# Attention in a two-layer backbone: p times v for four heads in one product, split into high and low parts

## The chip, the cores and the metric

The kernel runs on one core of a Trainium2 chip. The time is that of one execution on the device, in microseconds, as the median of several runs. The engines are named as the profile names them: PE is TensorE (matrix products and transposes into PSUM), PEld its loading of weights, DVE is VectorE, ACT is ScalarE, POOL is GpSimd, and SP issues most of the transfers. Each engine works through its own list of instructions in order and waits on semaphores of the others.

## The reference, cut to what matters

The program is one step of a backbone with two layers, for 128 context tokens and 256 latent tokens. Layer 0 is a gated MLP beside a state-space scan; layer 1, which the change touches, is grouped-query attention with 16 query heads, 4 key/value heads and heads of 128:

```python
def one_block(qblk):
    s = jnp.einsum('bqkgd,bskd->bkgqs', qblk, k).astype(jnp.float32) * scale
    p = jax.nn.softmax(s, axis=-1).astype(v.dtype)
    return jnp.einsum('bkgqs,bskd->bqkgd', p, v)
```

Context queries see the 128 context keys. Latent queries see 384 keys: 128 from a cache and 256 latent ones with rotary applied. The attention's output is multiplied by a SiLU gate z and goes through the output projection. Everything is fp32.

## The kernel before

Tokens are held as three tiles of 128 (t = 0 is the context, t = 1 and 2 the latents). The large products are done in fp32r in three parts: each fp32 operand is split into a high part (a copy to fp32r on ACT) and a low part (the difference, on DVE; `split`, line 274), and three products hi x hi, lo x hi, hi x lo are summed. Weights come as units of 128x1024 (`raw`), are split into `wh` and `wl` one or two units ahead of their use (`advance`, line 320), and four such pairs exist.

Layer 1 runs as follows. The keys' and values' projections come first. Then, for each of four groups g (one key/value head, four query heads), `xstat` does q's projection (512 columns per product) and `wstat` the gate z's (four units of 384 columns). The attention of the groups is worked in between: it is written as Python generators, and the planner runs one step of what is ready after every triple of projection products (`tick`, line 210), judged by a rough clock of its own that holds each engine's time; a step is taken 2.3 us of that clock after its inputs are due. The order in which steps are emitted is then kept on every engine.

One head of a (group, tile) pair is `head_gen` (line 1625): the scores on PE (`sm<-kT,qT`), the maximum on DVE (`mx`), the exponential with its sum on ACT (`p`), the reciprocal and the scaling on DVE, transposes of p on PE (`sm<-cm,p`, one per key block, so three for a latent tile and one for the context), a copy of them to SBUF on ACT (`pT`), and one fp32 product per key block on PE (`mm<-pT,vv`) into a quarter of a PSUM bank that the pair's four heads share (`po`). Up to three heads are under way at once (`attn_gen`). After the fourth head the bank is gated (`of<-mm,zs`, DVE) and split for the output projection (`aH` on ACT, `aL` on DVE).

Two places wait for the attention: the output projection may start once groups 0 to 2 are done, and its second block of columns takes its banks once group 3 is done (`until(...)` and `bank()` at the end of `build`). Where the planner must wait there, it goes on emitting steps of the attention with no projection product between them. Banks of PSUM: five for products (`mm`), three for scores and transposes (`sm`).

Of the kernel before, what the change touches and what calls it, by code (L numbers as in the profile page):

```python
# [8 lines left out]
F32 = mybir.dt.float32  # L9
F32R = mybir.dt.float32r  # L10
AF = mybir.ActivationFunctionType
# [5 lines left out]
P = 128  # L17
NT = 3
T = NT * P
# [156 lines left out]
def build(tc, A, O):  # L176
    nc = tc.nc
    clock = Clock()
    V, S, G, PE, SP = (Timed(e, n, clock) for e, n in (
        (nc.vector, "V"), (nc.scalar, "S"), (nc.gpsimd, "G"), (nc.tensor, "PE"), (nc.sync, "SP")))  # L180
    BF16 = mybir.dt.bfloat16
    with ExitStack() as ctx:
        def pool(name, bufs=1, space=None, st=ctx, **kw):
            if space is not None:
                kw["space"] = space
            return Slots(st.enter_context(tc.tile_pool(name=name, bufs=bufs, **kw)), name, bufs, clock)
# [17 lines left out]
        kept_bank = [0]  # L204
# [34 lines left out]
        def bank():  # L239
            until(lambda: live[0] + kept_bank[0] < MM)  # L240
            return any_bank()
# [5 lines left out]
        def free():  # L247
            live[0] -= 1

        def smt():  # L250
            until(lambda: sm_free)
            sm_free.remove(min(sm_free))
            return sm.tile([P, 512], F32, name="sm")

        def take():
            while not sm_free or min(sm_free) > clock.at["PE"] + SLACK:
                yield
            return smt()

        def give(ps):  # L260
            sm_free.append(clock.last(ps))
# [12 lines left out]
        def split(r, h, l):  # L274
            S.activation(h, r, AF.Copy)
            V.tensor_sub(l, r, h.bitcast(F32))
# [209 lines left out]
        def bc(ap, shape):  # L486
            return ap.to_broadcast(shape)
# [273 lines left out]
        while mod_at or w_at or rb or any(queue.values()):  # L761
# [3 lines left out]
            if xts:  # L765
                t, q = xts[0]
# [25 lines left out]
            elif what == "rb":  # L792
                b = min(rb)
# [405 lines left out]
        pss = [bank() for _ in range(NT)]  # L1199
# [3 lines left out]
        for q in range(1, 4):  # L1203
            pss = [bank() for _ in range(NT)]
# [33 lines left out]
        for n in range(4):  # L1238
            pss = [bank() for _ in range(NT)]
# [20 lines left out]
        for n in range(4):  # L1260
            pss = [bank() for _ in range(NT)]
# [55 lines left out]
        pss = [bank() for _ in range(NT)]  # L1317
# [26 lines left out]
        for n in range(1, 3):  # L1344
            pss = [bank() for _ in range(NT)]
# [61 lines left out]
        pss = {t: bank() for t in (0, 1)}  # L1407
# [27 lines left out]
        pss = {t: bank() for t in (0, 1)}  # L1435
# [35 lines left out]
        def k_norm(pl, t, ps):  # L1471
            ss = small.tile([P, 4], F32, name="ss")
            jk = pl.tile([P, P], BF16, name="jk", bufs=2 if pl is pb else 1)
            for h in range(4):
                S.activation(jk, ps[:, h * P:(h + 1) * P], AF.Square, accum_out=ss[:, h:h + 1])
            rk[t] = rstd(ss, P, 4)
# [22 lines left out]
        pk = pool("pk", 1, st=st)  # L1499
        pa = pool("pa", 1, st=st)  # L1500
        kT = pk.tile([P, 4, 4 * P], F32, name="kT")
        vv = pk.tile([P, 4, 512], F32, name="vv")
        SP.dma_start(out=kT[:, :, P:2 * P], in_=A["ckT"])
        SP.dma_start(out=vv[:, 1], in_=A["cv"])
        qkn = pk.tile([P, 2, P], F32, name="qkn")
        SP.dma_start(out=qkn, in_=A["qkn"].partition_broadcast(P))
        kq = pa.tile([P, 4, T], F32, name="zs", bufs=2)
# [1 line left out]
        def k_out(t, ps):  # L1509
            V.tensor_tensor(kq[:, :, t * P:(t + 1) * P], ps.rearrange("p (h c) -> p h c", h=4),  # L1510
                            bc(rk[t].unsqueeze(2), [P, 4, P]), op=ALU.mult)
            free()
# [5 lines left out]
        def make_tab():  # L1518
            rot = pa.tile([P, 2, 2, P], F32, name="of", bufs=1)
            SP.dma_start(out=rot, in_=A["rot"])  # L1520
            for w in (1, 0):
                G.tensor_tensor(tab[:, w, 0], rot[:, 0], bc(qkn[:, w].unsqueeze(1), [P, 2, P]), op=ALU.mult)
                q4 = qkn[:, w].rearrange("p (a b c) -> p a b c", a=2, b=2)
                for b in range(2):
                    G.tensor_tensor(tab[:, w, 1].rearrange("p t (a b c) -> p t a b c", a=2, b=2)[:, :, :, b],
                                    rot[:, 1].rearrange("p t (a b c) -> p t a b c", a=2, b=2)[:, :, :, b],
                                    bc(q4[:, :, 1 - b].unsqueeze(1), [P, 2, 2, 32]), op=ALU.mult)
                yield
# [26 lines left out]
        def k_seq(ps):  # L1555
            yield
            k_norm(pa, 2, ps)
            yield rk[2]
            k_out(2, ps)
            yield from make_tab()  # L1560
            yield tab
            for t in range(NT):
                c = 0 if t == 0 else (t + 1) * P
                yield from rope(kq[:, :, t * P:(t + 1) * P], t, 1, lambda: kT[:, :, c:c + P], ("k", t))
            flags.add("k done")
# [3 lines left out]
        def v1_gen(pss):  # L1569
            yield  # L1570
            for t in range(NT):
                S.activation(vv[:, 0 if t == 0 else t + 1], pss[t], AF.Copy)
                free()
            SP.dma_start(out=O[5], in_=vv[:, 0])
            flags.add("vv")

        pss = [bank() for _ in range(NT)]
# [42 lines left out]
            free()  # L1620
            flags.add(("z", g, h))

        heads, po, done = [0], {}, {}

        def head_gen(g, t, h):
            k0, nk = (0, 1) if t == 0 else (1, 3)
            w = nk * P
            ps = yield from take()
            PE.matmul(ps[:, :w], qT[g, t][:, h], kT[:, g, k0 * P:k0 * P + w], start=True, stop=True)
            if h == 3:  # L1630
                flags.add(("sc", g, t))
            mx = small.tile([P, 4], F32, name="mx", bufs=6)
            V.reduce_max(mx[:, 0:1], ps[:, :w], AX.X)
            V.tensor_scalar_mul(mx[:, 0:1], mx[:, 0:1], -scale)
            p = pa.tile([P, T], F32, name="p", bufs=3)
            S.activation(p[:, :w], ps[:, :w], AF.Exp, scale=scale, bias=mx[:, 0:1], accum_out=mx[:, 1:2])
            give(ps)
            yield p
            V.reciprocal(mx[:, 2:3], mx[:, 1:2])
            V.tensor_scalar_mul(p[:, :w], p[:, :w], mx[:, 2:3])  # L1640
            yield p
            pt = yield from take()
            for i in range(nk):
                PE.transpose(pt[:, i * P:(i + 1) * P], p[:, i * P:(i + 1) * P], ident)
            pT = pa.tile([P, 3, P], F32, name="pT", bufs=3)
            S.activation(pT[:, 0:nk], pt[:, :w].rearrange("p (a b) -> p a b", a=nk), AF.Copy)
            give(pt)
            yield pT
            if (g, t) not in po:
                while live[0] >= MM:  # L1650
                    yield
                po[g, t] = any_bank()
                kept_bank[0] = 0
                done[g, t] = 0
            for i in range(nk):
                PE.matmul(po[g, t][:, h * P:(h + 1) * P], vv[:, k0 + i, g * P:(g + 1) * P], pT[:, i],
                          start=i == 0, stop=i == nk - 1)
            heads[0] -= 1
            done[g, t] += 1
            if done[g, t] == 4:  # L1660
                while not has(*[("z", g, i) for i in range(4)]):
                    yield
                ts = slice(t * P, (t + 1) * P)
                of = pa.tile([P, 4, P], F32, name="of", bufs=1)
                V.scalar_tensor_tensor(of, po[g, t].rearrange("p (h c) -> p h c", h=4), 0.5,
                                       zst[g][:, :, ts], op0=ALU.mult, op1=ALU.mult)
                free()
                kept_bank[0] = int((3, NT - 1) not in po and all(x == 4 for x in done.values()))
                kept_bank[0] = int((3, NT - 1) not in po and len(po) == sum(x == 4 for x in done.values()))
                split(of, oH[:, 4 * g:4 * g + 4, ts], oL[:, 4 * g:4 * g + 4, ts])  # L1670
                flags.add(("attn", g, t))

        def attn_gen():
            while not has("vv", ("k", 0), ("k", 1), ("k", 2)):
                yield
            for g in range(4):
                for t in range(NT):
                    while ("q", g, t) not in flags:
                        yield
                    for h in range(4):  # L1680
                        while heads[0] >= 3:
                            yield
                        heads[0] += 1
                        spawn(head_gen(g, t, h))
                        yield
# [3 lines left out]
        for g in range(4):  # L1689
            pss = [bank() for _ in range(NT)]  # L1690
# [8 lines left out]
        pss = [bank() for _ in range(NT)]  # L1699
# [49 lines left out]
        pss = [bank() for _ in range(NT)]  # L1749
# [3 lines left out]
        pss = [bank() for _ in range(NT)]  # L1753
# [132 lines left out]
```

## Time and profile before

| | us |
|---|---|
| median of 3 runs | 1836.07 |
| lowest and highest run | 1833.1, 1837.0 |
| the profiled execution, its own time | 1834.68 |
| its span, first to last instruction | 1832.9 |
| PE busy in the span | 1776.6 |
| DVE busy | 1264.2 |
| ACT busy | 739.8 |

The mean granted clock of TensorE over the span is 0.991 of full speed. A busy time of PE is a sum of instructions whose ends are modelled, since products are pipelined; how long a product takes in a stream is better read from the distance between the starts of two that follow each other. In the timeline an fp32 product of 128 columns leaves two records.

### The profile page before, as it was taken

What the parts mean: (1) busy time and instruction counts of PE and PEld (TensorE: products, weight loads), DVE (VectorE), ACT (ScalarE), POOL (GpSimd) and SP (SyncE); (2) the same over time, 40 slices, a digit from 0 to 9 for tenths busy, and PEclk for the clock granted to TensorE, in tenths of its full rate; (3) what the DMA queues carried; (4) which work ended last, traced back from release to release, by engine and by line L of the source; (5) the groups of instructions that cost most, each with busy time, mean ns of one, the idle gap of its engine ahead of it and who ended that gap; (6) DMA issues with size and microseconds to landing.
All of it is one profiled execution on the core that took longest, in us unless ns stands there. A gap on an engine that the chain in (4) does not pass through costs nothing.

```text
span 1832.9 us, 24975 instructions
## 1 busy us (share of the span) xinstructions
PE 1776.6 (97%) x9332; PEld 1545.8 (84%) x9332; DVE 1264.2 (69%) x2023; ACT 739.8 (40%) x1380; POOL 203.4 (11%) x247
## 2 busy tenths in 40 slices
PE   6999998899999999999999999998999999999998
PEld 3579888899998888889999999877789898988876
DVE  4325888687768787777788878775566776776454
ACT  3224564566444332233233233244534344444441
POOL 0000134343222000000000000021311010000000
PEclk9999999999999999999999999999999999999999
DMA  9883455455434565776666656675454444434483
GB/s 359 340 309 128 140 171 160 126 146 154 153 127 138 183 205 170 224 213 206 214 204 210 209 188 210 216 243 195 148 190 154 138 150 150 149 127 149 138 286 116
DMA packets 109832, 340.86 MB, mean 186 GB/s; under 512 B 11920, under 2 KB 29840, under 8 KB 108560
## 3 DMA queue, kind: packets, MB, share of 16 engines
q1 hardware_dynamic: 109248, 339.18, 56.5%
q8 instruction: 73, 1.20, 0.3%
q14 instruction: 47, 0.39, 0.1%
q10 hardware_dynamic: 464, 0.10, 0.0%
HBM read 330.19 MB, written 9.04 MB: 185 GB/s over the span
## 4 chain that ended last, share of the span: by engine, by line
PE 83%; DVE 7%; ACT 3%; DMA 3%; issue 2%; POOL 1%; DVEq 0%; POOLq 0%; SPq 0%; ACTq 0%
PE mm L155 72%; PE sm L155 11%; DMA raw<-in_wout_dram 2%; DVE wl L155 2%; ACT wh L155 1%; DVE hb L155 1%; DVE acc L155 1%; DVE v L155 1%; DVE cv L155 1%; DMA raw<-in_mod_dram 0%; ACT hH L155 0%; ACT jk L155 0%; DMA gn<-gate 0%; DMA x<-in_x_dram 0%; DVE EE L155 0%
## 5 line engine op out<-in xcount | busy, mean ns | idle before, releaser
L155 DVE TENSOR_TENSOR wl<-raw,wh 128x1024 fp32r<-128x1024 f32 x358 | 440.7, 1238 | 301.8 <-ACT wh L155 301.2
L155 ACT ACTIVATE wh<-raw 128x1024 fp32r<-128x1024 f32 x358 | 375.7, 1056 | 488.2 <-DMA raw<-in_win_dram 195.0
L155 PE MATMUL mm<-hH,wh 128*128 128x384 f32 x1200 | 423.5, 353 | 3.8 <-DVE xpad L155 3.8
L155 PE MATMUL mm<-hH,wl 128*128 128x384 f32 x1200 | 404.3, 337 | 0.9 <-DVE wl L155 0.9
L155 PE MATMUL mm<-hL,wh 128*128 128x384 f32 x1200 | 403.7, 336 | 0.0
L155 DVE SCALAR_TENSOR_TENSOR acc<-raw,scol,acc 128x512 f32<-128x512 f32 x480 | 335.9, 760 | 15.1 <-DMA raw<-in_mod_dram 14.6
L155 PE MATMUL mm<-wh,hH 128*128 128x512 f32 x636 | 262.3, 412 | 6.1 <-DVE zs L155 4.0
L155 PE MATMUL mm<-wh,hL 128*128 128x512 f32 x636 | 249.7, 393 | 0.6 <-POOL hL L155 0.6
L155 PE MATMUL mm<-wl,hH 128*128 128x512 f32 x636 | 249.0, 392 | 0.0
L155 PEld LDWEIGHTS mm<-hH,wh 128*128 128x128 f32 x1200 | 227.1, 189 | 23.1 <-issue 20.5
L155 PEld LDWEIGHTS mm<-hL,wh 128*128 128x128 f32 x1200 | 227.2, 189 | 1.9
L155 PEld LDWEIGHTS mm<-hH,wl 128*128 128x128 f32 x1200 | 226.6, 189 | 2.1 <-DVE wl L155 2.1
L155 PE MATMUL mm<-wh,aL 128*128 128x512 f32 x504 | 196.6, 390 | 0.0
L155 PEld LDWEIGHTS mm<-wh,hH 128*128 128x128 f32 x636 | 120.3, 189 | 32.1 <-DVE zs L155 4.4
L155 PEld LDWEIGHTS mm<-wh,hL 128*128 128x128 f32 x636 | 119.9, 189 | 27.0 <-POOL hL L155 1.1
L155 PEld LDWEIGHTS mm<-wl,hH 128*128 128x128 f32 x636 | 120.4, 189 | 24.2
L155 PE MATMUL mm<-wl,r 128*128 128x512 f32 x348 | 136.2, 391 | 1.9 <-DVE wl L155 1.9
L155 PE MATMUL mm<-wh,r 128*128 128x512 f32 x348 | 136.8, 393 | 0.8 <-ACT wh L155 0.8
L155 POOL TENSOR_TENSOR rs_r<-rs_t,nhalf 128x1 f32<-128x1 f32 (+1 forms) x54 | 42.7, 791 | 642.1 <-DVE rs_t L155 641.8
L155 PEld LDWEIGHTS mm<-wh,aL 128*128 128x128 f32 x504 | 94.6, 188 | 19.6
L155 DVE SCALAR_TENSOR_TENSOR cv<-xpad,convw,cv 128x386 f32<-128x386 f32 x128 | 82.9, 651 | 2.3
L155 PEld LDWEIGHTS mm<-wl,r 128*128 128x128 f32 x348 | 65.3, 188 | 17.0 <-DVE wl L155 3.9
(257 smaller groups left out, 2084.4 us busy)
## 6 DMA issues: line engine op xcount, KB each, us to landing
raw<-in_win_dram SPq DMA_DIRECT2D x273, 512.0 KB, 4.0
raw<-in_mod_dram SPq DMA_DIRECT2D x128, 512.0 KB, 3.9
raw<-in_wout_dram SPq DMA_DIRECT2D x104, 512.0 KB, 4.3
aL<-in_mod_dram SPq DMA_DIRECT2D x52, 512.0 KB, 8.2
cb<-cumd SPq DMA_DIRECT2D x32, 384.0 KB, 5.5
wide<-in_mod_dram SPq DMA_DIRECT2D x12, 512.0 KB, 9.8
gn<-gate SPq DMA_DIRECT2D x8, 512.0 KB, 6.0
x<-in_x_dram SPq DMA_DIRECT2D x3, 1024.0 KB, 7.3
```

Of the source, the lines that this page charges most:

```text
L155: i = f(*a, **kw)
```

## The change

The probabilities of the four heads of one (group, tile) pair are transposed and split into `pH` and `pL`, which lie in one tile `[P, 2, 3, 4, P]`, heads side by side. Once all four are there, three fp32r products of 512 columns per key block give the whole bank. The values are kept as `vH` and `vL` in place of `vv`; the cached values are loaded into a scratch tile and split, and the context's values are copied once more for the output. There is one such pair of tiles, so the next pair's transposes come after the products of this one; there are two buffers of p in place of three, and two heads are under way at once in place of three. The program's scratch setting (`dynamic_dma_scratch_size`) goes from 4096 to 1024 bytes, which leaves more of SBUF for tiles.

```diff
-        vv = pk.tile([P, 4, 512], F32, name="vv")
+        vH = pk.tile([P, 4, 512], F32R, name="vH")
+        vL = pk.tile([P, 4, 512], F32R, name="vL")
-        SP.dma_start(out=vv[:, 1], in_=A["cv"])
+        cv = pa.tile([P, 512], F32, name="ro", bufs=1)
+        SP.dma_start(out=cv, in_=A["cv"])
...
+            yield cv
+            split(cv, vH[:, 1], vL[:, 1])
...
-                S.activation(vv[:, 0 if t == 0 else t + 1], pss[t], AF.Copy)
+                b = 0 if t == 0 else t + 1
+                split(pss[t], vH[:, b], vL[:, b])
+                if t == 0:
+                    vo = pa.tile([P, 512], F32, name="pT", bufs=1)
+                    S.activation(vo, pss[t], AF.Copy)
+                    SP.dma_start(out=O[5], in_=vo)
                 free()
-            SP.dma_start(out=O[5], in_=vv[:, 0])
...
-            p = pa.tile([P, T], F32, name="p", bufs=3)
+            p = pa.tile([P, T], F32, name="p", bufs=2)
...
+            if (g, t) not in pTs:
+                while pTs:
+                    yield
+                tl = pa.tile([P, 2, 3, 4, P], F32R, name="pT", bufs=1)
+                pTs[g, t] = tl[:, 0], tl[:, 1]
+                done[g, t] = 0
+            pH, pL = pTs[g, t]
             pt = yield from take()
             for i in range(nk):
                 PE.transpose(pt[:, i * P:(i + 1) * P], p[:, i * P:(i + 1) * P], ident)
-            pT = pa.tile([P, 3, P], F32, name="pT", bufs=3)
-            S.activation(pT[:, 0:nk], pt[:, :w].rearrange("p (a b) -> p a b", a=nk), AF.Copy)
+            split(pt[:, :w].rearrange("p (a b) -> p a b", a=nk), pH[:, 0:nk, h], pL[:, 0:nk, h])
             give(pt)
-            yield pT
-            if (g, t) not in po:
+            heads[0] -= 1
+            done[g, t] += 1
+            if done[g, t] == 4:
+                yield (pH[:, 0:nk], pL[:, 0:nk])
                 while live[0] >= MM:
                     yield
                 po[g, t] = any_bank()
                 kept_bank[0] = 0
-                done[g, t] = 0
-            for i in range(nk):
-                PE.matmul(po[g, t][:, h * P:(h + 1) * P], vv[:, k0 + i, g * P:(g + 1) * P], pT[:, i],
-                          start=i == 0, stop=i == nk - 1)
-            heads[0] -= 1
-            done[g, t] += 1
+                for i in range(nk):
+                    mh, ml = (x[:, i].rearrange("p h c -> p (h c)") for x in (pH, pL))
+                    wh, wl = (x[:, k0 + i, g * P:(g + 1) * P] for x in (vH, vL))
+                    PE.matmul(po[g, t], wh, mh, start=i == 0, stop=False)
+                    PE.matmul(po[g, t], wh, ml, start=False, stop=False)
+                    PE.matmul(po[g, t], wl, mh, start=False, stop=i == nk - 1)
+                del pTs[g, t]
...
-                        while heads[0] >= 3:
+                        while heads[0] >= 2:
...
-    nc = _bacc.Bacc("TRN2", target_bir_lowering=False, num_devices=1, dynamic_dma_scratch_size=4096)
+    nc = _bacc.Bacc("TRN2", target_bir_lowering=False, num_devices=1, dynamic_dma_scratch_size=1024)
```

The order of PE's instructions follows. Names: `hH`, `hL`, `aH`, `aL` are activations, `wh`, `wl` weights, `p` the probabilities (transposed against the identity `cm`), `qn` a rope's q on its way to `qT`, `mr` and `gcol` the gate vector of the layer's end.

The first place, on PE, is the passage from the last projection of q and z (products with `hH`) to the output projection (products with `aH`). In the kernel before it reads:

```order
L155 MATMUL sm<-cm,mr 128x128 x2
L155 MATMUL mm<-hH,wh 128x384
L155 MATMUL mm<-hL,wh 128x384
L155 MATMUL mm<-hH,wl 128x384
...
L155 MATMUL sm<-kT,qT 128x384
L155 MATMUL mm<-hH,wh 128x384
L155 MATMUL mm<-hL,wh 128x384
L155 MATMUL mm<-hH,wl 128x384
L155 MATMUL mm<-wh,aH 128x512
L155 MATMUL mm<-wl,aH 128x512
L155 MATMUL mm<-wh,aL 128x512
L155 MATMUL sm<-cm,qn 128x128 x4
```

In the changed kernel it reads:

```order
L155 MATMUL mm<-hH,wl 128x384
L155 MATMUL sm<-cm,p 128x128 x3
L155 MATMUL sm<-cm,qn 128x128 x4
L155 MATMUL sm<-cm,mr 128x128 x2
L155 MATMUL sm<-kT,qT 128x384
L155 MATMUL sm<-cm,p 128x128 x3
L155 MATMUL sm<-kT,qT 128x128
L155 MATMUL sm<-cm,gcol 32x128
L155 MATMUL sm<-cm,p 128x128 x3
L155 MATMUL sm<-kT,qT 128x128
L155 MATMUL sm<-cm,qn 128x128 x4
L155 MATMUL mm<-pT,vH 128x512 x2
```

Three heads of group 2's last tile now stand between the two projections, followed by that tile's nine products, where single steps stood between projection products.

The second place, on PE, is the end of the attention, after the first block of the output projection. In the kernel before:

```order
L155 MATMUL sm<-kT,qT 128x384
L155 MATMUL mm<-wh,aH 128x512
L155 MATMUL mm<-wl,aH 128x512
L155 MATMUL mm<-wh,aL 128x512
...
L155 MATMUL sm<-cm,p 128x128 x9
L155 MATMUL mm<-pT,vv 128x128 x9
L155 MATMUL mm<-wh,aH 128x512
```

In the changed kernel, from the last projection product to the first of tile 1's nine products:

```order
L155 MATMUL mm<-wh,aL 128x512
L155 MATMUL sm<-cm,p 128x128 x3
L155 MATMUL sm<-kT,qT 128x384
L155 MATMUL sm<-cm,p 128x128 x3
L155 MATMUL sm<-kT,qT 128x384
L155 MATMUL sm<-cm,p 128x128 x3
L155 MATMUL sm<-kT,qT 128x384
L155 MATMUL mm<-pT,vH 128x512 x2
L155 MATMUL mm<-pT,vL 128x512
```

And from there, after the rest of those nine, to the next projection product:

```order
L155 MATMUL sm<-cm,p 128x128 x3
L155 MATMUL sm<-kT,qT 128x384
L155 MATMUL sm<-cm,p 128x128 x3
L155 MATMUL sm<-kT,qT 128x384
L155 MATMUL sm<-cm,p 128x128 x6
L155 MATMUL mm<-pT,vH 128x512 x2
L155 MATMUL mm<-pT,vL 128x512
...
L155 MATMUL mm<-wh,aH 128x512
```

Three heads of tile 1 and all four of tile 2 now stand there, with both tiles' products, where the last tile's transposes and products stood.

## Rows read from the trace of the kernel before

**Rows 1.** The page's busy times: us (share of the span) xinstructions.
```profile
PE 1776.6 (97%) x9332; PEld 1545.8 (84%) x9332; DVE 1264.2 (69%) x2023; ACT 739.8 (40%) x1380; POOL 203.4 (11%) x247
```

**Rows 2.** Busy time of each engine in the attention's stretch.
```profile
core 0: us, PE busy (x) PEld busy (x) DVE busy (x) ACT busy (x) POOL busy (x), PEclk, DMA share, GB/s
1390.00:1713.80 323.80, 323.59 (x1796) 286.52 (x1794) 231.38 (x451) 141.94 (x322) 24.87 (x21) 1.00 0.43 142
```

**Rows 3.** Timeline of PE around two heads' products with v: start, us.
```profile
1409.11 0.38 PE L155 MATMUL mm<-pT,vv 128*128 128x128 f32 x2
1409.25 0.42 PE L155 MATMUL mm<-hH,wh 128*128 128x384 f32 x1
1409.51 0.34 PE L155 MATMUL mm<-hL,wh 128*128 128x384 f32 x1
...
1431.01 0.83 PE L155 MATMUL mm<-pT,vv 128*128 128x128 f32 x6
1431.59 0.47 PE L155 MATMUL mm<-wh,hH 128*128 128x512 f32 x1
1431.91 0.39 PE L155 MATMUL mm<-wl,hH 128*128 128x512 f32 x1
1432.14 0.39 PE L155 MATMUL mm<-wh,hL 128*128 128x512 f32 x1
```

**Rows 4.** Timeline of PE at the end of the attention.
```profile
1709.45 1.58 PE L155 MATMUL sm<-cm,p 128*128 128x128 f32 x9
1710.87 2.17 PE L155 MATMUL mm<-pT,vv 128*128 128x128 f32 x18
1712.80 0.47 PE L155 MATMUL mm<-wh,aH 128*128 128x512 f32 x1
...
1713.83 0.50 PE L155 MATMUL mm<-wh,aH 128*128 128x512 f32 x1
```

**Rows 5.** Groups 1390 to 1715 us: count | busy, mean ns | idle before, releaser.
```profile
L155 DVE TENSOR_TENSOR wl<-raw,wh 128x1024 fp32r<-128x1024 f32 x61 | 74.4, 1223 | 40.2 <-ACT wh L155 40.2
...
L155 ACT ACTIVATE wh<-raw 128x1024 fp32r<-128x1024 f32 x62 | 64.8, 1052 | 16.4 <-DMA raw<-in_win_dram 8.9 <-DMA raw<-in_wout_dram 5.5 <-PE mm L155 2.0
...
L155 ACT ACTIVATE pT<-sm 128x384 f32<-128x384 f32 x32 | 15.0, 487 | 22.9 <-PE sm L155 22.9
...
L155 DVE SCALAR_TENSOR_TENSOR zs<-zs,mm 128x384 f32<-128x384 f32 x16 | 8.7, 546 | 0.0
L155 DVE TENSOR_TENSOR aL<-of,aH 128x512 fp32r<-128x512 f32 x12 | 8.3, 692 | 8.4 <-ACT aH L155 8.4
...
L155 ACT ACTIVATE aH<-of 128x512 fp32r<-128x512 f32 x12 | 7.6, 632 | 34.8 <-DVE of L155 34.8
```

**Rows 6.** Timeline: steps of three heads on PE, DVE and ACT.
```profile
1670.62 0.81 PE L155 MATMUL sm<-kT,qT 128*128 128x384 f32 x2
...
1671.47 0.56 DVE L155 TENSOR_REDUCE mx<-sm 128x1 f32<-128x384 f32 x1 [0.92 <-PE sm L155]
...
1700.30 0.49 PE L155 MATMUL sm<-cm,p 128*128 128x128 f32 x3
...
1700.89 0.49 ACT L155 ACTIVATE pT<-sm 128x384 f32<-128x384 f32 x1 [0.54 <-PE sm L155]
...
1708.26 0.56 DVE L155 TENSOR_REDUCE mx<-sm 128x1 f32<-128x384 f32 x1
...
1709.95 0.42 DVE L155 TENSOR_SCALAR p<-p,mx 128x384 f32<-128x384 f32 x1
```

**Rows 7.** Three stretches with little work on PE or after it (columns as in Rows 2).
```profile
30.00:33.00 3.00, 0.56 (x2) 0.19 (x2) 2.14 (x3) 2.72 (x3) 0.00 (x0) 1.00 1.03 419
33.00:42.00 9.00, 8.64 (x34) 4.82 (x35) 1.17 (x2) 0.00 (x0) 0.00 (x0) 0.62 1.03 417
1752.00:1758.00 6.00, 2.77 (x9) 1.54 (x10) 2.81 (x3) 2.66 (x4) 0.00 (x0) 1.00 0.76 257
```

More of the change, by code (lines that the diff above doesn't have):

```diff
@@ L1621, in z_gen @@
             flags.add(("z", g, h))
-        heads, po, done = [0], {}, {}
+        heads, po, done, pTs, over = [0], {}, {}, {}, set()
         def head_gen(g, t, h):
@@ L1667, in head_gen @@
                 free()
-                kept_bank[0] = int((3, NT - 1) not in po and all(x == 4 for x in done.values()))
-                kept_bank[0] = int((3, NT - 1) not in po and len(po) == sum(x == 4 for x in done.values()))
+                over.add((g, t))
+                kept_bank[0] = int((3, NT - 1) not in po and len(po) == len(over))
                 split(of, oH[:, 4 * g:4 * g + 4, ts], oL[:, 4 * g:4 * g + 4, ts])
```

## The prediction

> **What bounds the kernel now.** I read the page's busy shares first, then TensorE (PE) over the attention stretch, then what one head costs on each engine, then the two places where the attention must be finished. PE is busy 97% of the span [rows 1]; from 1390 to 1713.8 us, where the attention runs between the projection products, it is busy 323.6 of 323.8 us, while VectorE (DVE) has 231.4 and ScalarE (ACT) 141.9 [rows 2]. So a product taken off PE shortens the run by its own time, work added to DVE or ACT is free while it stays behind PE, and a wait that stops PE is paid in full. In this stretch the attention's small steps lie singly between projection products, and the 0.2 us left over say that PE all but never waits for them.
>
> **The product of p and v on PE.** Before, one head of a latent tile is three fp32 products of 128 columns. In the stream this is the step from 1431.01 to 1431.59, and the product behind it starts its successor after 0.32 instead of 0.23 us [rows 3]: 0.58 + 0.09 = 0.67 us. A head of the context tile (one product) takes 0.14 + 0.08 = 0.22 us, where the next 384-wide products stand 0.26 apart [rows 3] against 0.23 x 384 / 512 = 0.17. With 32 latent and 16 context heads: 32 x 0.67 + 16 x 0.22 = 25.0 us. After, each of 12 (group, tile) pairs is one run of 512-wide products, three per key block: 8 x 9 + 4 x 3 = 84. These are products of the same kind as wh,hH, at 0.23 us from start to start [rows 3]: 84 x 0.23 = 19.3 us. The gain is **5.7 us**. Its bounds: heads that already stood side by side cost 0.64 instead of 0.67 (18 records in 1.93 us [rows 4]), which leaves about 4.7; with the switch between kinds of product saved in every case, not more than 6.5.
>
> **What is added beside PE.** ACT's copy of the transposed probabilities stays (487 ns [rows 5]) and now writes the high part. The low part is new on DVE: one subtraction per head that reads PSUM and SBUF. No such row exists; the nearest is the 384-wide step on zs with the same two sources, 546 ns [rows 5]. 32 x 0.55 + 16 x 0.28 (taken at half for a third of the columns) = 22 us. DVE goes from 231 to about 253 of 324 us. It also waits now for ACT's copy, and behind that wait stand the low parts of the weights (wl). They have cover: DVE spent 40 us of this stretch waiting for ACT before wl [rows 5]. I take 0, and keep 3 us for the high end. The parts of v add four pairs of copies and subtractions of 512 columns, 0.63 and 0.69 us each (by aH and aL [rows 5]), as the v products end; one PSUM bank is released later by some 0.7 us, which the six products ahead of its next use (6 x 0.23) cover. Nothing, at most 1.4 us. SP issues the same loads in the same order; v's load lands in a scratch tile, and the smaller scratch of the DMA setting costs no transfer here. Nothing.
>
> **What is moved: the order on PE.** Each (group, tile) now needs all four heads before its product, only one pair of pT tiles exists, and two heads run at once in place of three. So the attention falls behind the projections, and at the two places where the program must wait for it (all of groups 0 to 2 before the output projection starts, all of group 3 before its second block) several steps stand on PE with no projection product between them. The orders in the part on the change show this: before, one such place has nine transposes and nine products; after, the first has 10 steps of the attention and its neighbours and the second 14 steps with none between them. There the latency of a head is paid.
>
> That latency, from rows. Scores to the reduction: 1670.62 to 1671.47, 0.85 us. Reduction to scaled p: 1708.26 to 1709.95 + 0.42, 2.1 us [rows 6]. So **scores to p 3.0 us**. Transposes to ACT's copy: 1700.30 to 1700.89, 0.59 [rows 6]; copy 0.49, subtraction 0.55, hand-overs 0.1: **transposes to both parts 1.7 us**. A group's product is 9 x 0.23 = 2.1 us.
>
> *Second place* (t = 0 when the last projection product ends). Scores of tile 1's head 2 have just gone out, two triples and one score step earlier (2.0 us). PE does head 1's transposes and head 3's scores by 1.0. Head 2's p is scaled at 3.1, since DVE first subtracts head 1's low part and reduces head 3. Transposes, next scores: 4.1. Head 3's p is ready at 5.4 (behind head 2's subtraction), scores of tile 2's head 1 end at 6.5, and the copy of head 3 stands on ACT behind an exponential: its low part is there at 8.0. Product of tile 1: 8.0 to 10.05. Then DVE takes of (512 wide like aL, 0.69), waits for aH on ACT (0.63) and does aL (0.69) [rows 5] before it can subtract tile 2's head 0, so head 1's p comes at 13.5; scores of head 3 end at 14.6. Head 2's p 17.4, head 3's 19.7 (each behind a subtraction and a reduction), its parts at 21.4, product to 23.5, of to 24.4, when the bank is free: **24.5 us**. PE has work in it for 7 x 0.33 (transposes) + 5 x 0.65 (scores) + 18 x 0.23 = 9.7 us, so it idles 14.8. Before, the same place lasts from 1709.45 to 1713.83, 4.4 us [rows 4], with about 3.0 of work, 1.4 idle. Added: **13.4 us**.
>
> *First place.* ACT has a weight unit (wh, 1.05) and a zs step ahead of head 1's copy, DVE its own 1.22 (wl) for that unit [rows 5]. Scores of head 3 leave at 1.8 and end at 2.5, head 2's p at 4.1, the four small gcol steps and head 3's reduction follow, head 3's p at 8.1, its transposes and a rope's to 8.9, parts at 9.6, product to 11.7. PE has 5.7 us of work there (three sets of transposes, a long and two short scores, two rope sets, nine products). Before, these steps lay singly in the stream. Added: **6.0 us**.
>
> Sum: -5.7 + 13.4 + 6.0 = **+13.7 us**. The profiled execution took 1834.7 us (span 1832.9), 1.4 below the median of 1836.1; that is within the spread of the runs (1833.1 to 1837.0), so I add the sum to the median: **1850 us**. Later stages give nothing back: the output projection waits for its weight loads around 1752 to 1758 [rows 7], but the loads are held by buffers, not by the time since the start, so an earlier pause doesn't fill more of them.
>
> **Rivals.**
>
> *The clock falls.* In the second place PE works some 2.5 of the 11 us from 10.4 to 21.4. The trace has a stretch like it: from 30 to 33 us PE was busy 0.56 of 3, and over the next 9 us, with PE busy 8.64 of them, the granted clock read 0.62 on the mean, so it stood at 1.2 GHz for most of them: 9 x 0.38 = 3.4 us of full-speed work lost [rows 7]. From 1752 to 1758 PE was busy 2.77 of 6 and the clock stayed at 1.00, 2.4 GHz [rows 7]. The second place lies between these. If it falls: 1850 + 3.4 = 1853. The Trainium skill (TensorE: Matmul & The Clock Gate, "HAM oscillation — how this bites in real kernels") says that pauses between bursts of products bring the clock down again and that the next burst starts slow; by that rule 1853 is the likelier one, and the trace agrees at 33 us and disagrees at 1755.
>
> *DVE becomes the bound.* If a subtraction that waits for ACT's copy holds wl back by 1 us at each of the 12 pairs, 12 us more: 1862. For it: DVE at 253 of 324 us with a strict order. Against: the 40 us of waiting ahead of wl.
>
> *Faster.* The waits at the two places are short, because heads there are further on than I walk them. PE then keeps the gain: 1836.1 - 5.7 = 1830 with none of it lost. It decides at 5.7 us: if PE idles less than that in addition at the two places together, the change is a gain. Against it: at the second place scores of four heads follow one another by pairs, and two rounds of 3.0 + 1.7 us alone, with no queue at all, hold 9.4 us against 1.4 before.
>
> That the change doesn't do what it says can be left out: the order shows 84 products of 512 columns where 112 of 128 stood.
>
> **How the numbers follow.** Forecast 1850 (waits at both places, clock held): 0.50. Clock falls, 1853: 0.25. DVE bound, 1862: 0.07. Faster, 1830: 0.08. The remaining 0.10 is a half-sized wait: both places without queues on DVE and ACT give perhaps +5 us, 1841, and half of that case is within 0.2% (3.7 us, what a measurement of this kernel can tell from no change). So slower 0.87, same 0.05, faster 0.08. The range from 1841 to 1858 takes in the gain's bounds (1 us), the two walks at two thirds (-6.5), and the clock with the 3 us on DVE and 1.4 on v above; it leaves out 1862 and 1830.
>
> **What would show it.** After the change: 84 products pT,vH and pT,vL at 0.23 us pitch; PE idle some 15 us in one 25 us stretch with "DVE pT" and "DVE p" as what ended the waits, and some 6 us in one of 12 us that begins some 35 us before it; a granted clock below 1.00 in the first would be the clock rival; wl as what PE waits for in the rest of the stretch would be the DVE rival. The forecast is wrong if those two stretches show PE busy, or if PE waits in many small pieces elsewhere.

## The result and the profile after

The changed kernel took 1853.6 us (median; 1850.9 to 1855.6) where the kernel before took 1834.6 us in the same job: a ratio of 1.0101, 95% interval 1.0089 to 1.0113, so 19 us slower. The profiled execution has a span of 1853.8 us against 1832.9, 20.9 us more. The forecast was 1850 with a range from 1841 to 1858; it added 13.7 us to 1836.1, the median of the three runs known then.

The page's busy times answer to [rows 1], and the window over the attention's stretch answers to [rows 2] (same columns: PE, PEld, DVE, ACT, POOL, granted clock, DMA share, GB/s):

```profile
PE 1783.5 (96%) x9192; PEld 1541.6 (83%) x9192; DVE 1287.0 (69%) x2075; ACT 739.6 (40%) x1382; POOL 203.7 (11%) x247
```

```profile
1345.00:1663.00 318.00, 318.00 (x1649) 280.05 (x1648) 245.15 (x448) 132.61 (x302) 30.54 (x24) 1.00 0.49 158
...
1677.00:1704.00 27.00, 27.00 (x122) 21.67 (x121) 15.55 (x32) 11.73 (x22) 0.00 (x0) 1.00 0.39 132
```

PE has 140 instructions fewer and yet 6.9 us more busy time. From 1345 to 1663 us and again from 1677 to 1704 us it is busy in every microsecond, at the full clock, with DVE at 245 of 318 us. So nothing is lost in the long stretch in which the attention runs between projections; nearly all of what is lost lies in the two gaps between and behind these windows. They are the two places of the prediction.

**One pair's products in the stream**, on PE's timeline (start, length in us), answer to [rows 3]:

```profile
1653.86 0.34 PE L155 MATMUL mm<-hH,wl 128*128 128x384 f32 x1
1654.03 0.62 PE L155 MATMUL mm<-pT,vH 128*128 128x512 f32 x2
1654.48 0.39 PE L155 MATMUL mm<-pT,vL 128*128 128x512 f32 x1
...
1655.85 0.39 PE L155 MATMUL mm<-pT,vL 128*128 128x512 f32 x1
1656.07 0.34 PE L155 MATMUL mm<-hH,wh 128*128 128x384 f32 x1
```

Nine products take 1656.07 - 1654.03 = 2.04 us, 0.227 each, without a gap at either end.

**The first place**, PE's timeline with the wait and its releaser in brackets:

```profile
1663.38 0.34 PE L155 MATMUL mm<-hH,wl 128*128 128x384 f32 x1
1663.55 0.49 PE L155 MATMUL sm<-cm,p 128*128 128x128 f32 x3
...
1666.67 0.91 PE L155 MATMUL sm<-kT,qT 128*128 128x384 f32 x2 [1.02 <-DVE pT L155]
...
1669.56 0.28 PE L155 MATMUL sm<-cm,gcol 128*32 128x128 f32 x1 [1.01 <-ACT p L155]
1671.54 0.52 PE L155 MATMUL sm<-cm,p 128*128 128x128 f32 x3 [1.69 <-DVE p L155]
...
1672.83 1.20 PE L155 MATMUL mm<-pT,vH 128*128 128x512 f32 x2
...
1676.04 0.39 PE L155 MATMUL mm<-pT,vL 128*128 128x512 f32 x1
1676.27 0.39 PE L155 MATMUL mm<-wh,aH 128*128 128x512 f32 x1
```

It lasts from 1663.55 to 1676.27, 12.7 us. The same nine products that took 2.04 us in the stream take 3.44 here.

**The second place**, the same view; it answers to [rows 4]:

```profile
1704.70 0.39 PE L155 MATMUL mm<-wh,aL 128*128 128x512 f32 x1
1704.93 0.49 PE L155 MATMUL sm<-cm,p 128*128 128x128 f32 x3
...
1708.32 0.52 PE L155 MATMUL sm<-cm,p 128*128 128x128 f32 x3 [2.26 <-DVE p L155]
...
1710.63 0.88 PE L155 MATMUL sm<-cm,p 128*128 128x128 f32 x3 [1.14 <-DVE p L155]
...
1712.28 1.39 PE L155 MATMUL mm<-pT,vH 128*128 128x512 f32 x2
...
1716.45 0.55 PE L155 MATMUL sm<-cm,p 128*128 128x128 f32 x3
...
1719.91 0.82 PE L155 MATMUL sm<-cm,p 128*128 128x128 f32 x3 [2.26 <-DVE p L155]
...
1723.46 0.88 PE L155 MATMUL sm<-cm,p 128*128 128x128 f32 x3 [1.46 <-DVE p L155]
1726.13 0.87 PE L155 MATMUL sm<-cm,p 128*128 128x128 f32 x3 [1.79 <-DVE p L155]
1727.58 1.39 PE L155 MATMUL mm<-pT,vH 128*128 128x512 f32 x2 [0.58 <-ACT pT L155]
...
1731.75 0.63 PE L155 MATMUL mm<-wh,aH 128*128 128x512 f32 x1
```

From 1704.93 to 1731.75, 26.8 us. Five of the seven sets of transposes wait for a scaled p, 8.9 us in all; the two runs of nine products take 4.17 us each, twice the time they have in the stream.

**The clock**, in windows over both places and one later (columns as in [rows 2], the granted clock is the third number from the end):

```profile
1671.00:1674.00 3.00, 2.46 (x12) 2.25 (x13) 2.26 (x7) 1.01 (x5) 0.00 (x0) 0.70 0.02 5
...
1704.00:1707.00 3.00, 2.06 (x10) 1.22 (x8) 1.81 (x7) 1.05 (x3) 0.00 (x0) 1.00 0.11 44
1707.00:1710.00 3.00, 1.17 (x5) 0.58 (x5) 1.71 (x6) 1.16 (x3) 0.00 (x0) 0.96 0.00 0
1710.00:1713.00 3.00, 2.37 (x6) 1.46 (x7) 1.80 (x6) 1.05 (x3) 0.00 (x0) 0.50 0.00 0
...
1716.00:1719.00 3.00, 1.65 (x7) 0.81 (x5) 1.61 (x3) 1.01 (x2) 0.00 (x0) 0.90 0.01 3
1719.00:1722.00 3.00, 2.09 (x5) 0.98 (x5) 1.81 (x6) 1.05 (x3) 0.00 (x0) 0.66 0.00 0
1722.00:1731.00 9.00, 5.17 (x15) 3.54 (x15) 2.85 (x9) 1.65 (x4) 0.00 (x0) 0.50 0.01 2
1731.00:1734.00 3.00, 3.00 (x9) 2.31 (x8) 1.31 (x2) 1.28 (x2) 0.00 (x0) 0.56 0.00 0
...
1774.00:1780.00 6.00, 3.98 (x13) 2.64 (x12) 3.68 (x3) 3.17 (x3) 0.00 (x0) 0.83 0.63 208
1780.00:1786.00 6.00, 6.00 (x25) 4.88 (x24) 3.18 (x4) 3.64 (x5) 0.00 (x0) 0.88 0.75 251
```

At 0.50 PE runs at 1.2 GHz, its lower level. In the second place it is there for most of the time from 1710 to 1733: it came back as the first nine products ended (0.90 from 1716 to 1719), fell again among the single steps that follow, and was back at full speed by 1734. The last two rows are the output projection's wait for weights, the one that stood at 1752 to 1758 before [rows 7]: the idle time is the same, but this time the clock fell, which costs 6 x 0.17 + 6 x 0.12 = 1.7 us.

**DVE's groups** from 1340 to 1735 us (count | busy, mean ns | idle before, releaser) answer to [rows 5]:

```profile
L155 DVE TENSOR_TENSOR wl<-raw,wh 128x1024 fp32r<-128x1024 f32 x74 | 90.6, 1225 | 51.5 <-ACT wh L155 51.4
L155 DVE TENSOR_TENSOR pT<-sm,pT 128x384 fp32r<-128x384 f32 x32 | 17.7, 553 | 10.7 <-ACT pT L155 10.6
...
L155 DVE TENSOR_TENSOR pT<-sm,pT 128x128 fp32r<-128x128 f32 x16 | 4.5, 286 | 3.6 <-ACT pT L155 3.6
```

The subtractions take 553 and 286 ns, 22.2 us in all, and DVE waits 14.2 us for ACT's copies ahead of them, all without stopping PE outside the two places.

**Where the 20.9 us are.** Up to the second place the changed kernel is 4.5 us ahead (1704.93 against 1709.45). The second place lasts 26.8 us, where the one before took 3.35 to its first output product (1709.45 to 1712.80 [rows 4]): +23.5. From there to the end it is 122.05 against 120.1 us: +1.95. The output projection's first products run at the low clock there (six from 1731.75 to 1734.01, where the six before took from 1712.80 to 1714.63: 0.4 us more), and with the 1.7 above that explains all of it. -4.5 + 23.5 + 1.95 = 20.95.

Split by cause: the second place holds 9.7 us of PE's work at full speed (the prediction's count) against 3.0 before, so 17.1 of its 26.8 us are idle time or slow work, against 0.4 before: **+16.8**. The first holds 5.7, so 12.7 - 5.7 = **+7.0**. Behind them **+1.95**. The first scores start 0.8 us later (1397.97 against 1397.18). What is left is 20.95 - 16.8 - 7.0 - 1.95 - 0.8 = **-5.6**, the worth of the products. It is a remainder that rests on the prediction's counts of work, and the experiments below test it.

### The profile page after: what moved, and what is told of

Its sections match the earlier page's. It is cut to its first block, busy times and chain, and to the rows that moved or that the text cites. A ratio compares the mean times of both kernels' runs of the same rounds, so it can differ in the third digit from the quotient of the medians.

```text
span 1853.8 us, 24730 instructions
## 1 busy us (share of the span) xinstructions
PE 1783.5 (96%) x9192; PEld 1541.6 (83%) x9192; DVE 1287.0 (69%) x2075; ACT 739.6 (40%) x1382; POOL 203.7 (11%) x247
## 4 chain that ended last, share of the span: by engine, by line
PE 80%; DVE 10%; ACT 4%; issue 3%; DMA 2%; POOL 1%; DVEq 0%; POOLq 0%; SPq 0%; ACTq 0%
PE mm L155 70%; PE sm L155 10%; DVE wl L155 2%; DVE acc L155 2%; ACT wh L155 1%; DVE hb L155 1%; DMA raw<-in_mod_dram 1%; DMA raw<-in_wout_dram 1%; DVE v L155 1%; DVE cv L155 1%; ACT jk L155 1%; DVE mx L155 1%; DVE pT L155 0%; ACT hH L155 0%; DMA gn<-gate 0%
## 5 line engine op out<-in xcount | busy, mean ns | idle before, releaser
L155 PEld LDWEIGHTS mm<-wh,hL 128*128 128x128 f32 x636 | 120.1, 189 | 27.1 <-POOL hL L155 1.1
L155 PEld LDWEIGHTS mm<-wh,r 128*128 128x128 f32 x348 | 65.6, 188 | 16.0 <-issue 2.5
```

The lines of the kernel that those rows point to most:

```text
L155: i = f(*a, **kw)
```

## Experiments

Each experiment's time is compared with the kernel before in the same job (medians 1834.4 to 1836.6 us over the jobs), so the ratios are what to compare. The planner's delay is the line `now = clock.at["PE"] + SLACK` with SLACK = -2.3: a step of the attention is taken only 2.3 us of the planner's clock after its inputs are due. The diffs are against the kernel that the name begins with, in experiment 10 against experiment 9. Three questions: is the loss lateness in the plan, is the product worth what was said, and what does the clock cost?

**1. Two heads, and nothing else of the change.**

```diff
-            p = pa.tile([P, T], F32, name="p", bufs=3)
+            p = pa.tile([P, T], F32, name="p", bufs=2)
...
-                        while heads[0] >= 3:
+                        while heads[0] >= 2:
```

> The kernel before with one thing of the change: two heads under way at once and two buffers of p, the fp32 product per head kept. Theory (lateness): the limit of two heads alone makes the attention fall behind, and PE waits at the two places; its order has even more steps there than the changed kernel's, so 1834.6 + 20 to 28 = 1855 to 1862 us, with PE idle 5 to 8 us at the first place and 15 to 20 at the second. Rival (the split): the cause is the products kept back to the fourth head, or the new subtractions on VectorE; then the limit alone costs at most 3 us, so under 1838.

Measured: 1866.2 us, ratio 1.0169 (1.0154 to 1.0184). PE's waits from 1390 to 1750 us (in total, times, longest):

```profile
PE sm L155 <- DVE p L155: 11.1, 7, 3.2
PE sm L155 <- DVE mx L155: 3.2, 1, 3.2
PE mm L155 <- DVE qn L155: 2.6, 1, 2.6
```

Without a single split or 512-wide product the kernel is slower than the changed one. Two heads at a time alone make the attention late at the two places, where all of these waits lie but the one for `qn` (at 1474); the split is not needed for it. It lost more than I expected, 31 us beyond before by the ratio where up to 28 were expected, and with less idle time at the second place (8.9 us, where 15 to 20 were expected). So how the 31 us come about is only in part shown, and why it is more than in the changed kernel, beyond the 5 to 6 us of the product that it lacks, stays open.

**2. The changed kernel with no delay in the plan.**

```diff
-            now = clock.at["PE"] + SLACK
+            now = clock.at["PE"] + (0.0 if "vv" in flags else SLACK)
```

> The changed kernel with one number of the planner altered: from the values' projection on, a step of a generator may be emitted as soon as its inputs are due, in place of 2.3 us later. The order then has hardly any steps of the attention without projection products between them. Theory: the waits at the two places go with their clock loss (about 22 + 5 us), the gain of the 512-wide products (5 to 6 us) is left, and PE pays 0 to 4 us in small waits: 1829 to 1833 us. Rival (VectorE): the added subtractions cost in the stream, and the time stays above 1840 us.

Measured: 1837.7 us, ratio 1.0005 (0.9993 to 1.0017). All of the loss is gone with one number of the planner, so the products and the split are not what costs. The expected time was missed by some 5 us at its upper end. In part this is small waits of PE, 2.3 us for POOL's `qn`, 1.8 for DVE's `p` and 0.6 for ACT's `pT` from 1390 to 1750 us. The profiled execution took 1833.9 us, so its trace doesn't show what the median has beyond that.

**3. Half the delay.** The same line with -1.2.

> The changed kernel with the planner's delay at 1.2 us in place of 2.3 from the values' projection on. Its order has no run of steps at the first place, and at the second place one as long as before it. Theory: 7 us of waiting and 1.4 us of clock at the first place are gone, the second place stays: 1844 to 1847 us. Rival (the two waits are one delay that moves to wherever it ends): no gain, 1852 to 1854.

Measured: 1848.0 us, ratio 1.0058 (1.0038 to 1.0079). Its windows:

```profile
1650.00:1670.00 20.00, 19.83 (x117) 17.44 (x116) 16.33 (x34) 8.08 (x16) 1.29 (x1) 1.00 0.48 158
1670.00:1690.00 20.00, 20.00 (x94) 16.29 (x93) 11.95 (x29) 8.93 (x19) 0.00 (x0) 1.00 0.43 135
1690.00:1720.00 30.00, 20.51 (x74) 13.42 (x73) 16.34 (x43) 10.57 (x26) 0.00 (x0) 0.78 0.10 34
```

That is 1 us above what was expected, and below the rival. The first place is gone (PE busy 39.8 of 40 us), the second stands with its idle 9.5 us and its fallen clock. The two have separate prices, as the sum of the prediction had them: about 8 us less by the ratios (1.0101 - 1.0058) for the first, 7.0 by the trace.

**4. The second place filled.** At the second place, a useless 384-column product is issued at every other 0.2 us step of the planner's clock in which no step of the attention is ready (70 in all). It goes into a bank that the next block of the output projection starts afresh, and it leaves PE hardly any pause there.

```diff
+                        if fill[1] % 2 == 0:
+                            PE.engine.matmul(fill[0][:, :T], fill[2][:, 0, :P], fill[2][:, 1], start=True, stop=True)
```

> The changed kernel with products of no use put between the attention's steps at the second place, 71 of 384 columns into a bank that the next block starts afresh; the output is the same. Theory (clock): they keep the granted clock at 1.00 there, so both groups' products and the first output products take 0.23 in place of 0.43 us: 4 to 6 us less, 1848 to 1850. Rival: the lower clock in the records costs nothing, or the fillers take as long as they give back: 1853 or more.

Measured: 1850.5 us, ratio 1.0083 (1.0066 to 1.0099). The window over most of the second place, and its ends on PE's timeline (the products of no use stand in line 234):

```profile
1707.00:1731.00 24.00, 22.84 (x117) 19.00 (x116) 12.21 (x32) 8.18 (x19) 0.00 (x0) 1.00 0.00 1
```

```profile
1704.05 0.87 PE L234 MATMUL mm<-aH 128*128 128x384 f32 x4
...
1727.71 0.39 PE L155 MATMUL mm<-wh,aH 128*128 128x512 f32 x1
```

With more work on PE the kernel takes some 3.3 us less than the changed one by the ratios: the clock stays at 1.00, and the last steps run at full speed. The intervals overlap (this one's upper end is 1.0099, the other's lower 1.0089), so by the times alone the gain is not clear of noise. The trace is plainer: the clock stood, and the place lasts 23.7 us in place of 26.8, 3.2 less, with the 70 products in it. The rest of the place's loss remains, since waiting for the heads' chain on DVE and ACT is not shortened by it.

**5 and 6. Three heads in the changed kernel.** A third buffer of p is had from a half of the rope's table that is no longer read.

```diff
+        ps_free = [pa.tile([P, T], F32, name=f"p{n}") for n in range(2)]
+        ps_free.append(tab[:, 1].rearrange("p a b c -> p (a b c)")[:, :T])
...
-            p = pa.tile([P, T], F32, name="p", bufs=2)
+            p = ps_free.pop(0)
...
-                        while heads[0] >= 2:
+                        while heads[0] >= 3:
```

> The changed kernel with three heads under way at once, the planner's delay as it was. Its order has two scores and transposes of gate vectors beside nine products at the first place, and at the second four sets of transposes and two scores before the first nine products, then four sets of transposes and one score before the last nine. Theory: the first place's 7 us and its clock loss are gone, the second is shorter by a third: 1840 to 1845 us. Rival (the products kept back to the fourth head make it late by themselves): 1850 or more.

Measured: 1844.2 us, ratio 1.0042 (1.0026 to 1.0059), as expected: three heads take 11 us of the 19 back.

With three heads, and the delay at 1.0:

> The changed kernel with three heads under way at once again (the third buffer of p lies in the half of the rope table that is no longer used once the keys are done) and the planner's delay at 1.0 us in place of 2.3 from the values' projection on. Its order has one set of transposes and nine products at the second place and nothing at the first. Theory (lateness): the waits and the clock loss are gone and the gain of 5 to 6 us stays, less than 2 us of small waits since steps come a full us after they are due: 1829 to 1833 us, faster than the kernel before. Rival (VectorE holds the stream up through the subtractions): 1836 to 1842, as with no delay and two heads.

Measured: 1830.8 us, ratio 0.9977 (0.9969 to 0.9986), faster than both kernels and as expected. Its window over the attention and its busy times:

```profile
PE 1769.9 (97%) x9192; PEld 1534.7 (84%) x9192; DVE 1288.8 (71%) x2075; ACT 738.9 (40%) x1382; POOL 202.7 (11%) x247
```

```profile
1390.00:1704.00 314.00, 312.72 (x1627) 272.18 (x1625) 247.11 (x494) 138.24 (x320) 22.50 (x20) 1.00 0.44 145
```

PE is busy 312.7 of 314 us at the full clock, with the same subtractions on DVE (1288.8 us in all). Of waits for the attention two of 0.6 us are left, one for `qn` and one for `pT`.

**7. The kernel before with the smaller delay.** The control for the last: -1.0 in the same line, three heads and fp32 products as before (the text that follows says two heads; the edit leaves three).

> The kernel before with the planner's delay at 1.0 in place of 2.3 from the products of the first head on; two heads of three buffers and the fp32 product per head stay. Control for after_three_slack_1 (0.9977 of before). If the four-head product is worth 5 to 6 us, this is no faster than before: 1834 to 1839. If the smaller delay alone made that gain, it is 1829 to 1832.

Measured: 1835.8 us, ratio 1.0006 (0.9997 to 1.0015). So the smaller delay alone gains nothing, and against its control the four-head product is worth 1.0006 - 0.9977 = 0.0029, **5.3 us**; the two intervals leave it between 3 and 8. The two traces agree: from the first 384-wide product of layer 1 (`hH,wl`) to the 61st `wh,aH` product of the output projection they take 341.7 us with the four-head product (1380.96 to 1722.70) and 346.5 without it (1384.48 to 1731.02).

**8. The kernel before with no delay**, the control for 2:

> The kernel before with the planner's delay at 0 from the values' projection on, the counterpart of the run without delay of the changed kernel (1837.7 us). Theory (the product is worth 5 to 6 us, and steps without delay cost small waits in either kernel): 1841 to 1845 us. Rival (the 512-wide products give nothing in the stream): equal to that run, 1836 to 1839.

Measured: 1845.5 us, ratio 1.0064 (1.0049 to 1.0080). At no delay the changed kernel is better by 0.0059, 11 us, more than the product's own time. The plans differ in more than the product there (PE of this one waits 2.4 us for `zs` and 3.7 for `qn`), so 7 is the cleaner measure.

**9. The subtraction alone.** The kernel before with the low part's subtraction once per head, into a tile that nobody reads, and the smaller scratch.

```diff
+        low = pa.tile([P, 3, P], F32R, name="low")
...
+            V.tensor_sub(low[:, 0:nk], pt[:, :w].rearrange("p (a b) -> p a b", a=nk), pT[:, 0:nk])
```

> The kernel before with the low part of every head's transposed probabilities also computed on VectorE, into a tile that nothing reads; three heads at once, fp32 products. The planner sees the longer step too, and its order has 13 steps at the second place where the kernel before has two. Forecast of the prediction (hidden work): at most 3 us, under 1840. Theory of lateness: the subtraction lengthens each head's way in the plan, the attention ends late, and PE waits 8 to 12 us at the second place with some loss of clock: 1845 to 1850.

Measured: 1852.2 us, ratio 1.0090 (1.0077 to 1.0103). A step that my prediction had for nothing, 3 us at most, costs 16.5 us here, 2 more than the theory of lateness allowed. Its longest waits of PE from 1390 to 1750 us:

```profile
PE mm L155 <- DVE zs L155: 4.9, 1, 4.9
PE sm L155 <- DVE mx L155: 3.1, 2, 1.7
```

The waits come to 11 us, as that theory said, but not where it said: 3.9 of them lie at the second place, and 7.1 in the stream, the longest at 1648 us before a projection product. Two kinds of cost are mixed in the time: the planner counts the step, so its order is another one, and the chip does it.

**10. The same subtraction, not counted by the planner**, so that the order on PE is row for row that of before:

```diff
-            V.tensor_sub(low[:, 0:nk], pt[:, :w].rearrange("p (a b) -> p a b", a=nk), pT[:, 0:nk])
+            V.engine.tensor_sub(low[:, 0:nk], pt[:, :w].rearrange("p (a b) -> p a b", a=nk), pT[:, 0:nk])
```

> The kernel before with the low part's subtraction on DVE once per head, 128x2048 fp32, into a tile that nobody reads, issued so that the planner doesn't count it: TensorE's order is row for row that of the kernel before. The same work on DVE as in before_low_part (32 instructions of about 0.7 us each, some 22 us), without the lateness that the planner put into the order there. If that lateness is what before_low_part paid for (+16.5 us), this takes 1835 to 1839, at most 3 us over before, as the prediction held for a hidden subtraction. If it is DVE itself that runs late on the chip, it is 1845 to 1853 like before_low_part, and the waits of TensorE name DVE's p.

The text counts 32 instructions of 0.7 us; in the trace it is 32 of 0.55 and 16 of 0.29. Measured: 1841.9 us, ratio 1.0036 (1.0022 to 1.0049), +6.6 us: between the two theories. From 1345 to 1700 us PE never waits. Then its timeline at the end of the attention, where [rows 4] stood before:

```profile
1710.97 0.49 PE L155 MATMUL sm<-cm,p 128*128 128x128 f32 x3
1713.31 0.52 PE L155 MATMUL sm<-cm,p 128*128 128x128 f32 x3 [1.85 <-DVE p L155]
1715.67 0.52 PE L155 MATMUL sm<-cm,p 128*128 128x128 f32 x3 [1.85 <-DVE p L155]
1716.03 3.80 PE L155 MATMUL mm<-pT,vv 128*128 128x128 f32 x18
1719.58 0.48 PE L155 MATMUL mm<-wh,aH 128*128 128x512 f32 x1
```

The place takes 8.6 us in place of 3.35: two waits for p of 1.85 us, since DVE now has a subtraction ahead of each, and in front of it a wait of 1.2 to 1.3 us for ACT's copy, and then the products at half the clock (3.55 us in place of 1.93). So about 10 of the 16.5 us of experiment 9 go with the other order, and some 6 with the chip's own lateness at the one place where nothing covers DVE, clock included.

## Why the prediction came out as it did

The sign and the range held, and the time was 3.6 us from the forecast. As a difference the forecast was further off, 13.7 us against 19.0; the median that it was added to was 1.5 us higher than the one of the result. By its steps:

- **What bounds the kernel**: held. PE is busy in every microsecond of the stretch outside the two places, and waits at these are paid in full.
- **The product**: predicted 5.7 (4.7 to 6.5), measured 5.3 against the control in experiment 7. The remainder of the trace, 5.6, is not independent of the prediction, whose counts of work it uses. The pitch was 0.227 us, as taken from [rows 3].
- **The subtraction on DVE**: its work was right (22.2 us of 22). "I take 0" held for the stream, where PE never waits. At an uncovered place it is not nothing: the walk of the second place counted it there (each p stands behind a subtraction), and experiment 10 shows 3.7 us of such waits and their clock.
- **v's split and SP**: nothing, as predicted. PE is busy in every microsecond where the split lies, and the copies of v took 0.60 and 0.68 us.
- **The first place**: the walk gave 11.7 us, the trace 12.7. The added 6.0 became 7.0, but its make-up differs: the waits come to 4.5 us, and 1.4 more is the nine products at a lowered clock. That the sum came out near is in part luck.
- **The second place**: the walk gave 24.5 us, the trace 26.8. PE's idle time was shorter than walked (9.5 us of the 30 from 1704 to 1734, against 14.8), and its work slower (17.3 us for what takes 9.7): 4.3 in the two runs of products, the rest in transposes and scores and in the ends of pipelined steps that the trace counts as busy. For the place before, the prediction took 1.4 us of idle time; that was a wrong reading of [rows 4], whose 4.4 us hold three products of the output projection as well. By the count above 0.4 us are lost there, and the walk would have added 14.4 in place of 13.4.
- **Later stages**: they gave nothing back, as predicted, but they cost 1.95 us more, by the clock.

**The step that failed is the clock, taken as held.** The sum misses the measured profile by 20.9 - 13.7 = 7.2 us: 3.4 at the second place, 1.0 at the first, 1.95 behind them and 0.8 ahead of the attention. Counted by itself, the clock cost 1.4 in the first place's products, 4.3 in the second's, 0.4 behind them and 1.7 in the output projection's wait, 7.8 in all; the 1.0 us read wrongly in [rows 4] adds to the miss, and waits shorter than walked take from it. Experiment 4 tests the largest part: with the clock held, the second place lasts 23.7 us, close to the 24.5 of the walk. The forecast gave 0.50 to the held clock and 0.25 to the fallen one. The rival's 1853 comes out almost exactly, but not by its own working: it had 3.4 us at one place, and it was about twice that, at both places and behind them. What misled me was [rows 7]: a stretch from 1752 to 1758 with PE busy 2.77 of 6 us and the clock at 1.00. I read it as a stretch that holds the clock; in the kernels run here it does so in only half of the traces (below). In the second place PE was busy 1.17 of the 3 us from 1707 to 1710, and the clock stood at 0.50 from 1710.

The Trainium skill (TensorE: Matmul & The Clock Gate, "HAM oscillation — how this bites in real kernels") has pauses between bursts bring the clock down and the next burst start slow. The traces agree at both places of the changed kernel, where nine products take 3.44 us at the first and 4.17 at the second against 2.04 in the stream; the stretch from 1752 to 1758 of [rows 7], and its like in five other kernels, do not show it.

**The rivals.** DVE as the bound, with wl late, falls: PE waits for no wl in the stretch. The rival by which the kernel is faster, because the waits are short, falls for this plan. It is right for another one: the kernel of experiment 6 has hardly any such waits and is faster.

**What caused the waits**: two heads at once, and a planner that adds 2.3 us to each step of a chain that has become longer. Experiment 1 shows the first alone, 2 and 3 the second, 9 the third (a longer chain, with the order made late by it), and three heads with a delay of 1.0 remove all but 1.2 us of the waits. The prediction listed the one pair of pT tiles as a third cause. No run here tests it alone; with three heads and a delay of 1.0 the same one pair loses next to nothing, so it does not hold PE up by itself.

## What to carry to other kernels

A product made cheaper on the busy engine is worth its own time only if the work feeding it is not made late; count what the change takes from the number of chains under way, and walk the place where the program must wait for the last of them. Where a planner sets the order, its delay and its limits are part of the change: retune them with it, and run the old kernel with the same settings as a control. At a place where TensorE will idle in pieces, price its remaining work at half the clock too, and some of the work that follows, and treat a clock that held in one trace as a chance.

## What the runs showed of the hardware

The output projection's wait for weights is much the same in all twelve kernels profiled here, with one trace of each: 2.7 to 3.7 us of PE's time for `wh` and `wl`, in pieces of up to 1.9 us. In six of them the granted clock stayed at 1.00 through it, in the other six it fell, and the loss was 1.7 us each time (for example 0.72 over 6 us). No pattern by variant shows: the kernel before held it, and the same kernel with a delay of 1.0 lost it; the changed kernel lost it, and without the delay held it. One trace with a held clock is therefore no evidence that such a stretch holds it.

At this kernel's second place, giving TensorE useless work was cheaper than letting it rest: 70 products of 384 columns took the clock at the second place from 0.50 to 1.00 and the place from 26.8 us to 23.7; by the ratios, whose intervals overlap, the kernel became some 3 us faster.
